# Moving four of the sixteen transposes of x1 from the output projection to the last product, and turning the order of the accumulator banks by one

## The chip, the cores and the metric

The kernel runs on one core of one Trainium2 chip. The metric is the device time of one execution in microseconds (us); the median of three executions counts. TensorE multiplies matrices and appears in a profile as PE (the matmuls) and PEld (the weight loads, LDWEIGHTS, that precede each matmul). DVE is VectorE, ACT is ScalarE, POOL is GpSimd, SP is SyncE, which issues the loads.

## What is computed

The reference is one decoder layer over 256 rows of width 1024, in float32:

```python
h = rmsnorm(x, norm1_g)
proj = h @ w_in                      # queries, keys, values, gates
y_nsa, y_moba = ...                  # two attention mixers
gm = sigmoid(g_m)                    # two merge gates of 1024 columns each
mixed = g_nsa * (y_nsa @ w_up_nsa) + g_moba * (y_moba @ w_up_moba)
x = x + mixed @ w_out                # x1 in what follows
h2 = rmsnorm(x, norm2_g)
u = relu(h2 @ w_ff1)                 # 1024 -> 4096
x = x + (u * u) @ w_ff2              # 4096 -> 1024, the last product
return rmsnorm(x, norm_f_g)
```

## The kernel before

Every weight matrix is cut into chunks of 128 x 2048 float32 (1 MB), in the order of the table `CHUNKS`. SP loads a chunk into a `raw` buffer. ACT rounds it to `whi` (type float32r, line 107) and DVE takes the rest `wlo = raw - whi` (line 109). There are three buffers of each, and chunk c+2 is split while chunk c is multiplied. Activations are kept as such pairs too: `hTh`/`hTl`, `mxh`/`mxl`, `h2h`/`h2l`, `sqh`/`sql`. One product is three matmuls (`mm3`, line 214): high by high, high by low, low by high; all matmuls of the products stand on line 212.

Two forms of product matter here. In the input projection and the last product the activation is the weight load and 512 columns of `whi` or `wlo` stream past. In the output projection (`wstat` and `two_blocks`, chunks `C_WOUT`, four of them, called wout 0 to 3) and in ff1 (chunks `C_FF1`, sixteen) it is the other way round: 128 columns of `whi` or `wlo` are the weight load, and the 256 columns of `mxh`/`mxl` or `h2h`/`h2l` stream past. Such a chunk has 48 matmuls of 256 columns, 24 for each of its two output blocks. In the last product (ff2, sixteen chunks) a chunk has 24 matmuls of 512 columns; its two last chunks are worked together, and their last 24 matmuls have 256 columns.

The order on each engine is written by hand. `run_slot` walks through a chunk's matmuls, and events that `at(pos, f)` has put down are called when the share `pos` of them has been issued; on PE they stand between two matmuls, on the other engines behind what was called before.

PSUM has eight banks. Four belong to the score tiles, and later to the last product; `yb` is one; `acc0`, `acc1` and `tp` are three. `tp` takes transposes up to the chunk before the merge gates: its last use is the second half of the keys `km`, which DVE reads last (line 312, `split_evac`). From the gates on it is one of three accumulators: `next_bank` (line 63) takes the first name of the list `turn["acc"]` and puts it at the end.

In wout 1 and in the second chunk of the last product, x1, which is held transposed as `x1T`, is turned back into rows by `x1_rows` (line 768): for each of four pairs of row blocks four 128 x 128 transposes on PE (line 773) into one bank, and one copy by ACT into `x1` (line 775). `rstd2` reads `x1` two chunks later.

Of the kernel before, what the change touches and what calls it, by code (L numbers as in the profile page):

```python
# [40 lines left out]
def hybrid_layer(ctx: ExitStack, tc: tile.TileContext, gxd, w, w1c, small, const, gf, out):  # L41
# [16 lines left out]
    def bank(tag, name):  # L58
        return ps.tile([128, 512], F32, name=name, tag=tag)

    turn = {"acc": ["acc0", "acc1"], "tp": ["tp", "yb"]}

    def next_bank(kind):
        t = turn[kind]
        t.append(t.pop(0))
        return bank(t[-1], kind)

    def acc_tile():
        return next_bank("acc")
# [6 lines left out]
    def s_tile(x):  # L76
        if "s" not in pools:
            early_stack.close()
            pools["s"] = at_stack.enter_context(tc.tile_pool(name="ps_s", bufs=1, space=PS))
        return pools["s"].tile([128, 2, 512], F32, name="S" + "ab"[x])  # L80
# [113 lines left out]
    def at(pos, f, *a):  # L194
        ev.append((pos, f, a))

    def run_slot(mms):
        n = len(mms)
        es = sorted(ev, key=lambda e: e[0])
        ev.clear()  # L200
        j = 0
        for i, m in enumerate(mms):
            while j < len(es) and es[j][0] <= i / n:
                es[j][1](*es[j][2])
                j += 1
            m()
        while j < len(es):
            es[j][1](*es[j][2])
            j += 1
# [24 lines left out]
    def wstat(o, c, off, nk, ncol, ah, al, ks=None, first=0, last=None):  # L234

        r = []
        last = nk - 1 if last is None else last
        for k in (range(nk) if ks is None else ks):
            a = k * ncol + off
            r += mm3(o, hi[c][:, a:a + 128], lo[c][:, a:a + 128], ah[:, k, :], al[:, k, :],  # L240
                     k == first, k == last)
        return r

    def split_events(c, hs, ls):
        for i in range(2):
            at(hs[i], split, c + 2, i, 2, "h")
        for i in range(2):
            if ls[i] <= 1:
                at(ls[i], split, c + 2, i, 2, "l")
        if ls[1] <= 1:  # L250
            at(max(ls) + 0.05, load, c + 5)

    def std_events(c):
        if 9 <= c < 20 and c % 2:
            split_events(c, (0.0, 0.06), (0.09, 0.46))
        elif 9 <= c < 20:
            split_events(c, (0.0, 0.45), (0.3, 0.8))
        else:
            split_events(c, (0.0, 0.45), (0.3, 0.46))
# [377 lines left out]
                       scale=hrstd[:, t:t + 1])  # L637

    prev = []
    turn["acc"].append("tp")  # L640
    for g in range(4):
        accs = [acc_tile(), acc_tile()]
        for i in range(2):
# [28 lines left out]
    def mix_t(t, i, tp):  # L672
        for j in range(4):
            pe.transpose(tp[:, j * 128:(j + 1) * 128],
                         sgs[0][:, t, (4 * i + j) * 128:(4 * i + j + 1) * 128], ident)
        k, q = mix_slices(t, i)
        U["mx", t, i] = tp.rearrange("p (j q) -> p j q", j=4)
        act.activation(mxh[:, k, q], U["mx", t, i], AF.Copy, scale=0.5)
# [35 lines left out]
    def two_blocks(c, ah, al, late=8):  # L714

        if late < 8:
            outs = [acc_tile()[:, 0:256] for _ in range(2)]
            whole = None
            order = [range(late), range(late, 8)]
        else:  # L720
            whole = acc_tile()
            outs = [whole[:, 0:256], whole[:, 256:512]]
            order = [range(8)]
        mms = []
        for ks in order:
            for m in range(2):
                mms += wstat(outs[m], c, m * 128, 8, 256, ah, al, ks=ks, last=7)
        return mms, outs, whole
# [34 lines left out]
    def lo_late(pos, c):  # L763
        for k in range(2):
            at(pos, split, c + 2, k, 2, "l")
        at(pos + 0.01, load, c + 5)

    def x1_rows(k2s, tiles):
        for k2, tp in zip(k2s, tiles):
            v = tp.rearrange("p (t d) -> p t d", t=2)  # L770
            for t in range(2):
                for m in range(2):
                    pe.transpose(v[:, t, m * 128:(m + 1) * 128],
                                 x1T[:, 2 * k2 + m, t * 128:(t + 1) * 128], ident)
            act.activation(FB["x1"][:, :, k2 * 256:(k2 + 1) * 256], v, AF.Copy)

    for i in range(4):
        c = C_WOUT + i
        if i == 0:
            at(0.03, lambda: mix_t(0, 1, bank("yb", "yb")))  # L780
            at(0.04, mix_l, 0, 1)
            at(0.29, lambda: mix_t(1, 1, s_tile(1)[:, 0]))
            at(0.3, mix_l, 1, 1)
            lo_late(0.35, c - 1)
        elif i == 1:
            lo_late(0.03, c - 1)
        split_events(c, (0.0, 0.1), ((9, 9), (0.3, 0.3), (0.3, 0.3), (9, 9))[i])
        for f, a in prev:
            at(0.02, f, *a)
        if i == 1:  # L790
            at(0.01, open_ff)

            at(26 / 48 - 0.001, lambda: x1_rows([0], [bank("yb", "yb")]))
            at(0.9, lambda: act.dma_start(FB["gfb"], gf[None, :].to_broadcast([128, 1024])))
        if i == 3:
            outs = [acc_tile()[:, 0:256] for _ in range(2)]
            at(0.52, wout_evac, i, outs, (0,))
            run_slot([m for j in range(2)
                      for m in wstat(outs[j], c, j * 128, 8, 256, mxh, mxl)])
            prev = [(wout_evac, (i, outs, (1,)))]  # L800
        else:
            mms, outs, _ = two_blocks(c, mxh, mxl, 4 if i == 0 else 8)
            run_slot(mms)
            prev = [(wout_evac, (i, outs))]
# [46 lines left out]
    def ff2_mms(i, p):  # L851
        c = C_FF2 + i
        t, c0, n = p
        r = []
        for k in range(2):
            kt = 2 * i + k
            lh, ll = (FB[a][:, kt, t * 128:(t + 1) * 128] for a in ("sqh", "sql"))
            a = k * 1024 + c0
            r += mm3(ops[p][:, 0:n], lh, ll, hi[c][:, a:a + n], lo[c][:, a:a + n],
                     kt == (28 if p == LAST[1] else 0),  # L860
                     kt == (27 if p == PARTS[1][1] else 31))
        return r
# [35 lines left out]
    for i in range(15):  # L898
        std_events(C_FF2 + i)
        for f, a in prev:  # L900
            at(0.02, f, *a)
        prev = []
        if i == 1:
            at(0.5, x1_rows, range(1, 4), [acc_tile() for _ in range(3)])
        if i == 3:
            at(0.1, rstd2)
        if i < 14:
            run_slot([m for p in order for m in ff2_mms(i, p)])
        else:
            ops[LAST[1]] = bank("yb", "yb")  # L910
            at(0.05, first_part)
            at(0.23, final_a, PARTS[0][0], 0)
            at(0.43, final_a, PARTS[0][1], 1)
            at(0.46, final_b, 0)
            at(0.64, final_a, PARTS[1][0], 0)
            at(0.83, final_a, LAST[0], 1)
            run_slot([m for p in PARTS[0] + PARTS[1][:1] + LAST for m in ff2_mms(14, p) + ff2_mms(15, p)])
# [87 lines left out]
```

## Time and profile before

| | |
|---|---|
| median of three executions | 386.05 us (385.52 to 386.81) |
| the profiled execution | 386.25 us, span 384.4 us |
| PE, matmuls | 375.2 us busy, 98% of the span |
| PEld, weight loads | 329.1 us, 86% |
| DVE | 254.3 us, 66% |
| ACT | 205.6 us, 54% |

The span runs from the first to the last instruction of the program, and 1.85 us lie outside it. A busy PE need not be PE at its peak: matmuls overlap, and a matmul's duration is longer than the distance between the starts of two. That distance is called the pitch below, and it is what a stream of matmuls costs.

### The profile page before, as it was taken

The page shows a single profiled execution, that of the slowest core. Times are in us where ns is not written, and L with a number is a line of the kernel's source. Part 1 is how long each engine was busy: PE and PEld are TensorE (multiplying, and loading weights), DVE is VectorE, ACT ScalarE, POOL GpSimd, SP SyncE. Part 2 cuts the span into 40 slices and gives each one's busy share as a digit, 9 for nine tenths or more (in the row PEclk, how much of TensorE's full clock was granted, in tenths as well). Part 3 has the DMA queues.
Part 4 walks back from the last instruction along what each step waited for, and adds up shares of the span by engine and source line. Part 5 has one row for each costly group of instructions (what it writes and reads, how often), then busy time and mean ns, then how long its engine had stood idle before and what let it go on. Part 6 is the DMA issues. An engine that isn't in the chain of part 4 may idle for free.

```text
span 384.4 us, 5939 instructions
## 1 busy us (share of the span) xinstructions
PE 375.2 (98%) x2404; PEld 329.1 (86%) x2404; DVE 254.3 (66%) x396; ACT 205.6 (54%) x359; POOL 3.2 (1%) x14
## 2 busy tenths in 40 slices
PE   7999999999999999999999999999999999999993
PEld 6897778878888788779999999999998888888883
DVE  3969788887966869567857656756757354344435
ACT  5974465766746747353554555565565364323412
POOL 1000000000000000000000000000000000000000
PEclk9999999999999999999999999999999999999999
DMA  7977535333533434630756644554564546545003
GB/s 243 368 304 231 208 124 205 109 111 124 206 109 112 124 140 175 217 112 7 264 224 219 220 160 175 215 188 155 206 213 143 206 186 237 198 162 188 0 2 110
DMA packets 11261, 66.31 MB, mean 173 GB/s; under 512 B 1249, under 2 KB 2785, under 8 KB 3937
## 3 DMA queue, kind: packets, MB, share of 16 engines
q1 hardware_dynamic: 10800, 65.14, 47.5%
q10 hardware_dynamic: 432, 0.79, 0.6%
q8 instruction: 19, 0.31, 0.3%
q14 instruction: 10, 0.07, 0.1%
HBM read 64.87 MB, written 1.05 MB: 172 GB/s over the span
## 4 chain that ended last, share of the span: by engine, by line
PE 90%; DVE 3%; ACT 2%; issue 2%; DMA 1%; SPq 1%; POOLq 0%; POOL 0%; DVEq 0%; ACTq 0%
PE acc L212 54%; PE o L212 21%; PE qacc L212 3%; PE yb L212 3%; PE kvbacc L212 2%; DMA raw<-in_kva_dram 1%; DVE wlo L109 1%; PE Sa L212 1%; PE Sa L493 1%; PE Sb L493 1%; ACT whi L107 1%; PE tp L293 1%; PE Sb L212 1%; PE tp L212 1%; DVE hTl L168 0%
## 5 line engine op out<-in xcount | busy, mean ns | idle before, releaser
L107 ACT ACTIVATE whi<-raw 128x1024 fp32r<-128x1024 f32 (+2 forms) x128 | 123.2, 991 | 99.6 <-PE o L212 35.5
L109 DVE TENSOR_TENSOR wlo<-raw,whi 128x1024 fp32r<-128x1024 f32 (+2 forms) x128 | 141.6, 1137 | 43.8 <-ACT whi L107 43.6
L212 PE MATMUL acc<-h2h,whi 128*128 128x256 f32 x256 | 71.9, 281 | 0.0
L212 PE MATMUL acc<-h2l,whi 128*128 128x256 f32 x256 | 71.9, 281 | 0.0
L212 PE MATMUL acc<-h2h,wlo 128*128 128x256 f32 x256 | 71.9, 281 | 0.0
L212 PE MATMUL acc<-whi,hTh 128*128 128x512 f32 (+1 forms) x128 | 51.2, 400 | 0.9 <-ACT whi L107 0.5
L212 PE MATMUL acc<-wlo,hTh 128*128 128x512 f32 (+1 forms) x128 | 51.1, 399 | 0.4 <-DVE wlo L109 0.2
L212 PE MATMUL acc<-whi,hTl 128*128 128x512 f32 (+1 forms) x128 | 49.8, 389 | 0.0
L212 PE MATMUL o<-whi,sqh 128*128 128x512 f32 (+1 forms) x128 | 49.5, 386 | 0.0
L212 PE MATMUL o<-whi,sql 128*128 128x512 f32 (+1 forms) x128 | 49.4, 386 | 0.0
L212 PE MATMUL o<-wlo,sqh 128*128 128x512 f32 (+1 forms) x128 | 49.4, 386 | 0.0
L212 PEld LDWEIGHTS acc<-h2h,wlo 128*128 128x128 f32 x256 | 49.2, 192 | 0.0
L212 PEld LDWEIGHTS acc<-h2h,whi 128*128 128x128 f32 x256 | 48.1, 188 | 0.0
L212 PEld LDWEIGHTS acc<-h2l,whi 128*128 128x128 f32 x256 | 48.1, 188 | 0.0
L212 PEld LDWEIGHTS acc<-whi,hTh 128*128 128x128 f32 x128 | 24.3, 190 | 7.9 <-ACT whi L107 1.3
L212 PEld LDWEIGHTS acc<-wlo,hTh 128*128 128x128 f32 x128 | 24.3, 190 | 5.4 <-DVE wlo L109 1.5
L212 PEld LDWEIGHTS o<-whi,sql 128*128 128x128 f32 x128 | 24.0, 188 | 4.9
L212 PEld LDWEIGHTS o<-wlo,sqh 128*128 128x128 f32 x128 | 24.1, 188 | 4.8
L212 PEld LDWEIGHTS o<-whi,sqh 128*128 128x128 f32 x128 | 24.0, 188 | 4.7
L212 PEld LDWEIGHTS acc<-whi,hTl 128*128 128x128 f32 x128 | 24.4, 190 | 4.2
L816 DVE TENSOR_TENSOR ur<-ur 128x512 f32<-128x512 f32 x16 | 11.1, 693 | 20.6 <-ACT ur L815 19.4
L818 DVE TENSOR_TENSOR sql<-ur,sqh 128x512 fp32r<-128x512 f32 x16 | 11.1, 692 | 11.2 <-ACT sqh L817 11.2
(245 smaller groups left out, 513.5 us busy)
## 6 DMA issues: line engine op xcount, KB each, us to landing
raw<-in_ff_dram SPq DMA_DIRECT2D x32, 1024.0 KB, 4.8
raw<-in_gm_dram SPq DMA_DIRECT2D x8, 1024.0 KB, 4.8
raw<-in_wout_dram SPq DMA_DIRECT2D x4, 1024.0 KB, 4.8
raw<-in_q_dram SPq DMA_DIRECT2D x2, 1024.0 KB, 5.9
raw<-in_qm_dram SPq DMA_DIRECT2D x2, 1024.0 KB, 5.3
raw<-in_km_dram SPq DMA_DIRECT2D x2, 1024.0 KB, 4.9
raw<-in_vm_dram SPq DMA_DIRECT2D x2, 1024.0 KB, 4.8
raw<-in_upn_dram SPq DMA_DIRECT2D x2, 1024.0 KB, 4.8
```

What stands on the lines that cost most here:

```text
L107: act.activation(hi[c][:, a:b], raw[c][:, a:b], AF.Copy)
L109: dve.tensor_tensor(lo[c][:, a:b], raw[c][:, a:b], hi[c][:, a:b].bitcast(F32), op=ALU.subtract)
L212: pe.matmul(o, l, r, start=start, stop=stop, skip_group_check=True)
L293: pe.transpose(tp[:, j * 256 + t * 128:j * 256 + t * 128 + 128], src[:, t, (2 * i + j) * 128:(2 * i + j + 1) * 128], ident)
L493: pe.transpose(S[x][:, j, c:c + 128], P[:, 2 * x + j, c:c + 128], ident)
L816: dve.tensor_tensor(rf, rf, rf, op=ALU.mult)
L818: dve.tensor_tensor(l, rf, h.bitcast(F32), op=ALU.subtract)
```

## The change

Three edits. The bank `tp` is put at the front of the list of accumulators instead of at its end, so that the first accumulator of the gates is in `tp`, and each later one in the bank that the accumulator before it had. The call of `x1_rows` in wout 1 goes. The call in the second chunk of the last product makes all four pairs, the last of them in the bank `yb`.

```diff
     prev = []
-    turn["acc"].append("tp")
+    turn["acc"].insert(0, "tp")
     for g in range(4):
...
         if i == 1:
             at(0.01, open_ff)
-
-            at(26 / 48 - 0.001, lambda: x1_rows([0], [bank("yb", "yb")]))
             at(0.9, lambda: act.dma_start(FB["gfb"], gf[None, :].to_broadcast([128, 1024])))
...
         if i == 1:
-            at(0.5, x1_rows, range(1, 4), [acc_tile() for _ in range(3)])
+            at(0.5, x1_rows, range(4), [acc_tile() for _ in range(3)] + [bank("yb", "yb")])
         if i == 3:
             at(0.1, rstd2)
```

PE where the gates begin, with the engine whose work each matmul waits for in brackets; `acc_961` is the first gates' accumulator, `acc_797` the last one of the values before it. Before:

```order
L212 MATMUL acc_797<-wlo_707,hTh_129 128x512
L212 MATMUL acc_797<-whi_706,hTl_130 128x512
L212 MATMUL acc_961<-whi_798,hTh_129 128x512 [waits Activation_49]
L212 MATMUL acc_961<-wlo_799,hTh_129 128x512
L212 MATMUL acc_961<-whi_798,hTl_130 128x512
```

Now:

```order
L212 MATMUL acc_797<-wlo_707,hTh_129 128x512
L212 MATMUL acc_797<-whi_706,hTl_130 128x512
L212 MATMUL acc_961<-whi_798,hTh_129 128x512 [waits DVE_49]
L212 MATMUL acc_961<-wlo_799,hTh_129 128x512
L212 MATMUL acc_961<-whi_798,hTl_130 128x512
```

No matmul has moved: the first one of the gates waits for DVE, where it waited for ACT.

PE in wout 1, at the start of its second block. Before:

```order
L212 MATMUL acc_1763<-mxh_1501,wlo_1651 128x256
L212 MATMUL acc_1763<-mxh_1501,whi_1650 128x256
L212 MATMUL acc_1763<-mxl_1502,whi_1650 128x256
L773 MATMUL yb_1826<-ident_72,gx_107 128x128 [waits DMAHW0_49,DVE_49]
L773 MATMUL yb_1826<-ident_72,gx_107 128x128 [waits DVE_49]
L773 MATMUL yb_1826<-ident_72,gx_107 128x128 x2
L212 MATMUL acc_1763<-mxh_1501,wlo_1651 128x256
L212 MATMUL acc_1763<-mxh_1501,whi_1650 128x256
L212 MATMUL acc_1763<-mxl_1502,whi_1650 128x256
```

Now the four transposes (`gx` holds x1T) are gone, and the chunk's 48 matmuls follow each other without a break, as those of wout 2, wout 3 and ff1 do before and now. PE in the second chunk of the last product, now:

```order
L212 MATMUL o0_512_2972<-whi_2910,sql_1781 128x512
L773 MATMUL acc_3012<-ident_72,gx_107 128x128 [waits DMAHW0_49,PE_49]
L773 MATMUL acc_3012<-ident_72,gx_107 128x128 x3
L773 MATMUL acc_3013<-ident_72,gx_107 128x128 [waits DMAHW4_49,PE_49]
L773 MATMUL acc_3013<-ident_72,gx_107 128x128 x3
L773 MATMUL acc_3014<-ident_72,gx_107 128x128 [waits DMAHW6_49,Activation_49]
L773 MATMUL acc_3014<-ident_72,gx_107 128x128 x3
L773 MATMUL yb_3015<-ident_72,gx_107 128x128 [waits DMAHW0_49]
L773 MATMUL yb_3015<-ident_72,gx_107 128x128 x3
L212 MATMUL o1_0_2973<-whi_2910,sqh_1780 128x512
```

Here sixteen transposes stand in a row between two 512-column matmuls, where there were twelve.

## Rows read from the trace of the kernel before

**Rows 1.** The profile's page, part 4: the chain that ended last, by engine.

```profile
PE 90%; DVE 3%; ACT 2%; issue 2%; DMA 1%; SPq 1%; POOLq 0%; POOL 0%; DVEq 0%; ACTq 0%
```

**Rows 2.** The chain of waits in order of time: start us, us, what.

```profile
31.00 1.99 PE tp L212 x64
...
179.08 5.85 PE acc L212 x49
184.93 0.44 PE yb L773 x4
185.36 104.35 PE acc L212 x886
...
297.88 1.31 PE acc L773 x12
299.19 73.48 PE o L212 x324
```

**Rows 3.** Timeline where the gates begin: start us, us, engine, line, operation [idle before].

```profile
85.40 0.68 DVE L312 TENSOR_TENSOR kml<-tp,kmh 128x512 fp32r<-128x512 f32 x1
...
85.56 0.39 PE L212 MATMUL acc<-whi,hTl 128*128 128x512 f32 x1
85.57 0.72 ACT L273 ACTIVATE vm<-acc,rstd 128x512 f32<-128x512 f32 x1
...
86.34 0.50 PE L212 MATMUL acc<-whi,hTh 128*128 128x512 f32 x1 [0.40 <-ACT vm L273]
```

**Rows 4.** Timeline of ACT in the last product's second chunk.

```profile
298.35 1.58 ACT L775 ACTIVATE x<-acc 128x512 f32<-128x512 f32 x3 [1.10 <-PE acc L773]
```

**Rows 5.** Timeline of PE in wout 1, around its transposes.

```profile
181.81 0.28 PE L212 MATMUL acc<-mxh,whi 128*128 128x256 f32 x1
...
184.53 0.28 PE L212 MATMUL acc<-mxh,whi 128*128 128x256 f32 x1
...
184.76 0.60 PE L773 MATMUL yb<-ident,gx 128*128 128x128 f32 x4
```

**Rows 6.** Groups of instructions, 179.7 to 184.6 us: xcount | busy us, mean ns.

```profile
L212 PE MATMUL acc<-mxh,wlo 128*128 128x256 f32 x15 | 4.1, 276 | 0.0
...
L212 PEld LDWEIGHTS acc<-mxh,wlo 128*128 128x128 f32 x15 | 2.8, 188 | 0.0
```

**Rows 7.** Groups of instructions, 199.2 to 289.2 us (ff1).

```profile
L212 PE MATMUL acc<-h2h,wlo 128*128 128x256 f32 x255 | 71.7, 281 | 0.0
L212 PEld LDWEIGHTS acc<-h2h,wlo 128*128 128x128 f32 x255 | 49.0, 192 | 0.0
...
L212 PEld LDWEIGHTS acc<-h2h,whi 128*128 128x128 f32 x255 | 47.9, 188 | 0.0
```

**Rows 8.** Busy us (xcount) of PE, PEld, DVE, ACT, POOL by stretch, granted clock, DMA.

```profile
181.00:184.60 3.60, 3.60 (x34) 3.60 (x33) 2.25 (x6) 2.70 (x4) 0.00 (x0) 1.00 0.60 189
...
240.00:245.00 5.00, 5.00 (x45) 5.00 (x44) 3.65 (x4) 2.48 (x4) 0.00 (x0) 1.00 0.57 213
```

**Rows 9.** Timeline of PE in wout 0, behind its second group of transposes (line 674).

```profile
177.07 0.60 PE L674 MATMUL Sb<-ident,sga 128*128 128x128 f32 x4
...
177.63 0.28 PE L212 MATMUL acc<-mxh,whi 128*128 128x256 f32 x1
...
178.65 0.28 PE L212 MATMUL acc<-mxh,whi 128*128 128x256 f32 x1
```

**Rows 10.** Timeline at the start of ff1, PE and DVE.

```profile
199.10 0.28 PE L212 MATMUL acc<-h2h,whi 128*128 128x256 f32 x1
...
200.30 0.48 DVE L759 SCALAR_TENSOR_TENSOR h2l<-gx,h2h 128x256 fp32r<-128x256 f32 x1 [0.58 <-ACT h2h L756]
...
200.70 1.22 DVE L109 TENSOR_TENSOR wlo<-raw,whi 128x1024 fp32r<-128x1024 f32 x1
```

**Rows 11.** Timeline of PE in the last 24 matmuls of the last product.

```profile
375.57 0.28 PE L212 MATMUL o<-whi,sqh 128*128 128x256 f32 x1
...
377.97 0.28 PE L212 MATMUL yb<-whi,sql 128*128 128x256 f32 x1
```

## The prediction

> **What bounds the kernel now.** I read the chain of waits first. PE holds 90% of it, DVE 3%, ACT 2% and loads 1% [rows 1]; so the time is what PE's stream costs, plus a few gaps. From 185.36 us on the chain is nothing but PE until the end of the last product: 886 matmuls, 36, twelve transposes, 324 [rows 2]. In this part no wait is to be had, and only a cheaper matmul can shorten it. Two places matter. The first is a gap where the gates begin. The second is the price of one matmul in wout and ff1, which I read as a pitch (start to start), since durations overlap.
>
> That price has two values for the same instruction. In wout 1, before its transposes, 24 matmuls lie between the start at 181.81 and the start at 184.53: 2.72 / 24 = 113.3 ns each [rows 5]. Behind the four transposes the chain has 886 matmuls in 104.35 us: 117.78 ns each [rows 2]. The count is exact: 22 left of wout 1, 48 in each of wout 2 and 3, 48 in each of sixteen chunks of ff1. The 512-column matmuls of the last product cost 73.48 / 324 = 226.8 ns, twice the lower value, so 113.3 is the rate of the stream and the other 4.4 ns are a loss. It is no matter of TensorE's clock: the granted clock is 1.00 (2.4 GHz) in a stretch at either pitch, and DVE, ACT and loads are busy in both [rows 8]. The weight loads tell more. At the lower pitch a load of `wlo` takes 188 ns and the matmul 276 [rows 6]; at the higher one the load of `wlo` takes 192, that of `whi` still 188, the matmul 281 [rows 7]. One load in three meets something in every round, and this has settled: it is there from the transposes to the end of ff1, whatever buffer is read. I take it for two steady states of the same stream, loads and streamed columns in step or out of step, and the transposes for what throws it from the one into the other.
>
> **The change part by part, against the profiled execution (386.25 us; the median is 0.20 lower).**
>
> *The gates' first accumulator.* Before, the last matmul of the values starts at 85.56, and the next was due a pitch later, at 85.79. It starts at 86.34, because ACT empties its bank only from 85.57 to 86.29 [rows 3]: a gap of 0.55 us. Now it waits for DVE's read of the keys in `tp`, 85.40 to 86.08 [rows 3]. With the same 0.05 us from end to start it begins at 86.13, a gain of 0.21 us. What stands in front of that read on DVE is not touched. Bounds: 0 if DVE runs 0.21 us later than in this execution, 0.55 if the read is done before PE comes. The second accumulator waits for the copy that ends at 86.29 and is due twelve pitches (2.7 us) after the first, so it is covered; all later accumulators only change names. PE's lead meets no load on the chain later, so I count it whole: -0.21.
>
> *The transposes on PE.* Four go, 0.44 us of the chain, and four come, in a row with twelve that take 1.31 us, 0.109 us each [rows 2]: -0.44 + 0.44 = 0. On ACT one copy moves along, behind the three of the last product, 1.58 / 3 = 0.53 us each [rows 4]. They stand between the roundings of two chunks, and what hides the fourth is the rest of the chunk on PE, twelve matmuls of 226.8 ns, 2.7 us; without that cover it would cost at most its 0.53 us, once. The `yb` bank is idle there, and `rstd2` comes two chunks later. The load of the last gain vector is issued on ACT a little earlier, without the copy before it, and is used only at the end. All nothing.
>
> *The pitch.* If the stream stays at 113.3 ns through the rest of wout and through ff1, 886 x (117.78 - 113.33) = 3.94 us go. No row shows ff1 at the lower pitch, so I bound it: from above by this 3.94, from below by a loss, if the stream goes to the pitch of the last product's 256-column matmuls. There 20 lie between 375.57 and 377.97, 120.0 ns each [rows 11], and 886 x 2.2 = 2.0 us would be added. I take the upper end, by the nearest row: the same matmuls with the same operands as the 22 next, directly before them, with nothing between. In wout the good state crosses a seam unharmed: it is there from 179.7 on, in wout 0, and wout 1 begins at 181.81 with other buffers and another bank [rows 5, 6].
>
> Against it: transposes alone don't decide the state. Behind the second group in wout 0 nine steps from 177.63 to 178.65 take 1.02 us, 113.3 ns again [rows 9]. So there is chance in how a break ends, and a later break could do what this one did. I find none: the 22 + 96 + 768 matmuls stand in one row, and what feeds them is early. The last `h2l` ends at 200.78 [rows 10], 1.7 us after ff1 begins; it is wanted 36 matmuls in, 4.1 us at the lower pitch. The next chunk's `wlo` comes from the first two of the splits from 200.70 on, 1.22 us each [rows 10]; both are done 4.0 us after ff1's start and are wanted from 5.4 us on. A chunk of ff1 would take 48 x 113.3 ns = 5.44 us, just what a chunk of the last product takes now (24 x 226.8 ns) with the same 1 MB load. DVE, 3.65 of 5 us busy in ff1 [rows 8], would be at 76%.
>
> The Trainium skill, "TensorE: Matmul & The Clock Gate", section "Step-by-step: what each phase is for", speaks against this: PE has two independent read ports in SBUF, so that loading the next weights takes nothing from the running matmul. By it, load and stream could not disturb each other, the 4.4 ns would have a cause that the transposes don't touch, and the sum would be the first rival's. The trace does not agree as far as it shows: the load of `wlo` is 4 ns longer exactly where the matmul is 5 ns longer [rows 6, 7].
>
> Sum: 386.25 - 0.21 - 3.94 = 382.10 for the profiled execution, **381.9 us** against the median.
>
> **The rivals.**
>
> 1. *The pitch stays at 117.8.* The transposes only happen to stand where the stream leaves its short good stretch; or it falls back at the next seam, at the latest where `h2h` takes the place of `mxh`. For: the good state is seen for at most the 49 matmuls before the transposes [rows 2], and never with `h2h`. Against: its stretch ends at the transposes to the matmul, not at a seam. Left is the gap at the gates: 386.05 - 0.21 = 385.8; if only wout keeps the lower pitch, (22 + 96) x 4.45 ns = 0.5 us more go, 385.3. Here the change does little of what it could.
>
> 2. *PE's queue feeds it no faster.* Two instructions per 117.78 ns, 58.9 each, would be the limit, and the quicker stretches would live off what was stored in a wait. That too gives 385.8. Against it: 64 matmuls with their 64 loads pass in 1.99 us at 31.0 us [rows 2], 15.5 ns per instruction. The skill's same page, section "Wait — 56ns, not 53.3ns?", states about 62 ns per matmul for one way of decoding; the 1.99 us exclude that here.
>
> 3. *The stream stays good into ff1 and falls back in the middle of it:* 382.5 to 384.9.
>
> 4. *Slower: the stream settles at 120 ns*, the third value, which the last product's final matmuls take up within three matmuls, without any transposes [rows 11]. It decides at the first seam behind wout 1's first half. 886 x 2.2 ns = 2.0 us more, less 0.21: 387.8. Against: there the roles are others, the activation is the load and `whi` streams, and all three loads are slow, not one.
>
> **How the numbers follow.** Forecast 0.64; rival 1 0.21; rival 2 0.03; rival 3 0.06; rival 4 0.06. A measurement can tell about 0.3%, 1.16 us, from no change: faster means below 384.9. The forecast and rival 3 lie there: 0.70. Rivals 1 and 2 are no change: 0.24. Rival 4 is slower: 0.06. The range reaches from 381.2 (the forecast, 0.34 more at the gates if DVE is done early, and 0.4 for the spread of a median between 385.5 and 386.8) to 386.1 (rivals 1 and 2 with the gain at the gates at 0), and leaves out rival 4. The forecast's own range is 381.2 to 382.5.
>
> **What would show it.** Right: the chain's 864 matmuls of wout 2, wout 3 and ff1, if not more, cost 113.3 ns each, their loads of `wlo` take 188 ns and the matmuls 276; the gates' first matmul follows DVE's read of `kml` with about 0.35 us of gap left; sixteen transposes take some 1.75 us in the last product. Wrong: `wlo` loads of 192 ns in ff1 (rival 1), in all three loads (rival 4), or a wait for `whi`, `wlo` or a load inside ff1, which would say that the quicker stream outruns what feeds it.

## The result, and the profile after

| | before | after |
|---|---|---|
| median | 385.64 us (385.50 to 386.81, 6 executions) | 381.88 us (381.43 to 382.69, 6 executions) |
| ratio, 95% interval | | 0.9893 [0.9876, 0.9910] |
| the profiled execution | 386.25 us, span 384.4 us | 382.69 us, span 380.8 us |

Faster by 1.1%, more than three times what a measurement can tell from no change; 381.9 us had been forecast. The chain of waits of the changed kernel, in order of time (start us, us, what), answers to [rows 2]:

```profile
178.72 0.70 DVE mxl L682
179.43 0.04 issue
179.47 106.25 PE acc L212 x935
285.72 8.18 PE o L212 x36
293.90 1.31 PE acc L773 x12
295.21 0.44 PE yb L773 x4
295.65 73.48 PE o L212 x324
```

Where there were 49 matmuls, four transposes and 886 matmuls, there are 935 matmuls in a row. From the end of the wait for `mxl` to the first matmul of the last product PE needs 106.25 us, where it needed 5.85 + 0.44 + 104.35 = 110.64 [rows 2]. Of the 4.39 us that are gone, 0.44 are the four transposes, which come back at 295.21, and 3.95 are a cheaper matmul. The 36 and 324 matmuls of the last product cost what they did. Groups of instructions in ff1, 199 to 286 us (xcount | busy us, mean ns of one), which answer to [rows 7]:

```profile
L212 PE MATMUL acc<-h2h,wlo 128*128 128x256 f32 x256 | 70.7, 276 | 0.0
...
L212 PEld LDWEIGHTS acc<-h2l,whi 128*128 128x128 f32 x255 | 47.9, 188 | 0.0
L212 PEld LDWEIGHTS acc<-h2h,wlo 128*128 128x128 f32 x255 | 47.9, 188 | 0.0
L212 PEld LDWEIGHTS acc<-h2h,whi 128*128 128x128 f32 x254 | 47.7, 188 | 0.0
```

All loads take 188 ns; the `wlo` load of 192 ns is gone, and with it the matmul of 281. The clock has no part in it, as before: the stretches 180 to 198 and 200 to 284 us (busy us and count of PE, PEld, DVE, ACT, POOL, then the granted clock, the DMA share and GB/s) stand at 1.00 (2.4 GHz), and 84 us hold 744 matmuls, those that overlap the edges among them, where [rows 2] stand for 84 / 0.11778 = 713:

```profile
180.00:198.00 18.00, 18.00 (x161) 18.00 (x160) 14.22 (x22) 9.06 (x13) 0.00 (x0) 1.00 0.75 264
200.00:284.00 84.00, 84.00 (x744) 84.00 (x743) 57.39 (x64) 48.46 (x63) 0.00 (x0) 1.00 0.56 196
```

The timeline where the gates begin answers to [rows 3]:

```profile
85.98 0.68 DVE L312 TENSOR_TENSOR kml<-tp,kmh 128x512 fp32r<-128x512 f32 x1
...
86.14 0.39 PE L212 MATMUL acc<-whi,hTl 128*128 128x512 f32 x1
86.16 0.72 ACT L273 ACTIVATE vm<-acc,rstd 128x512 f32<-128x512 f32 x1
...
86.72 0.50 PE L212 MATMUL acc<-whi,hTh 128*128 128x512 f32 x1 [0.18 <-DVE kml L312]
```

The first matmul of the gates was due at 86.14 + 0.23 = 86.37, waits for DVE's read of `tp` and starts at 86.72: a gap of 0.35 us, where it was 0.55. The profiled execution is still 0.6 us longer than the 382.10 worked out for it. This lies ahead of the stretch above, whose start is 0.39 us later than before and not 0.21 earlier. PE's list of waits names what came in between: before, one wait of 0.5 us for a rounding to `whi`; in this execution,

```profile
PE acc L212 <- ACT whi L107: 1.4, 2, 0.9
PE acc L212 <- DVE kml L312: 0.2, 1, 0.2
PE acc L212 <- DVE mxl L682: 0.2, 1, 0.2
```

(us in total, times, longest). The chain shows this rounding at 77.20 us, in a part that the change does not touch; it varies between executions, and 382.69 is the longest of the six.

### The profile page after: what moved, and what is told of

It reads as the page before. It is cut to its first block, busy times and chain, and to the rows that moved or that the text cites. A ratio compares the mean times of both kernels' runs of the same rounds, so it can differ in the third digit from the quotient of the medians.

```text
span 380.8 us, 5938 instructions
## 1 busy us (share of the span) xinstructions
PE 370.8 (97%) x2404; PEld 324.8 (85%) x2404; DVE 254.3 (67%) x396; ACT 205.7 (54%) x359; POOL 3.2 (1%) x14
## 4 chain that ended last, share of the span: by engine, by line
PE 87%; DVE 5%; ACT 2%; issue 2%; DMA 1%; SPq 1%; POOLq 0%; POOL 0%; DVEq 0%; ACTq 0%
PE acc L212 52%; PE o L212 21%; PE kvbacc L212 2%; PE yb L212 2%; DVE wlo L109 2%; PE qacc L212 2%; ACT whi L107 2%; DMA raw<-in_kva_dram 1%; PE Sa L493 1%; PE Sb L493 1%; PE Sa L212 1%; PE tp L212 1%; PE Sb L212 1%; PE tp L293 1%; DVE hTl L168 0%
## 5 line engine op out<-in xcount | busy, mean ns | idle before, releaser
L212 PE MATMUL acc<-h2h,whi 128*128 128x256 f32 x256 | 70.7, 276 | 0.0
L212 PE MATMUL acc<-h2l,whi 128*128 128x256 f32 x256 | 70.7, 276 | 0.0
L212 PE MATMUL acc<-h2h,wlo 128*128 128x256 f32 x256 | 70.7, 276 | 0.0
L212 PE MATMUL acc<-whi,hTh 128*128 128x512 f32 (+1 forms) x128 | 50.8, 397 | 1.6 <-ACT whi L107 1.4
L212 PE MATMUL acc<-wlo,hTh 128*128 128x512 f32 (+1 forms) x128 | 50.7, 396 | 0.4 <-DVE wlo L109 0.2
L212 PE MATMUL o<-whi,sqh 128*128 128x512 f32 (+1 forms) x128 | 49.5, 386 | 0.0
L212 PE MATMUL acc<-whi,hTl 128*128 128x512 f32 (+1 forms) x128 | 49.4, 386 | 0.0
L212 PE MATMUL o<-whi,sql 128*128 128x512 f32 (+1 forms) x128 | 49.4, 386 | 0.0
L212 PE MATMUL o<-wlo,sqh 128*128 128x512 f32 (+1 forms) x128 | 49.4, 386 | 0.0
L212 PEld LDWEIGHTS acc<-h2h,whi 128*128 128x128 f32 x256 | 48.1, 188 | 0.0
L212 PEld LDWEIGHTS acc<-h2l,whi 128*128 128x128 f32 x256 | 48.1, 188 | 0.0
L212 PEld LDWEIGHTS acc<-h2h,wlo 128*128 128x128 f32 x256 | 48.1, 188 | 0.0
L212 PEld LDWEIGHTS acc<-whi,hTh 128*128 128x128 f32 x128 | 24.1, 189 | 8.4 <-ACT whi L107 2.1
L212 PEld LDWEIGHTS acc<-wlo,hTh 128*128 128x128 f32 x128 | 24.1, 188 | 5.4 <-DVE wlo L109 1.6
L212 PEld LDWEIGHTS o<-whi,sql 128*128 128x128 f32 x128 | 24.0, 188 | 4.9
L212 PEld LDWEIGHTS o<-wlo,sqh 128*128 128x128 f32 x128 | 24.0, 188 | 4.8
L212 PEld LDWEIGHTS o<-whi,sqh 128*128 128x128 f32 x128 | 24.0, 188 | 4.8
L212 PEld LDWEIGHTS acc<-whi,hTl 128*128 128x128 f32 x128 | 24.1, 188 | 4.2
```

Of the source, the lines that this page charges most:

```text
L212: pe.matmul(o, l, r, start=start, stop=stop, skip_group_check=True)
```

## Experiments

Below, **quick** is a stream of 256-column matmuls at 113.3 ns from start to start, **slack** one at 117.8 ns, and a **break** is whatever stands between two such matmuls: a wait, or transposes. The question was whether the transposes alone make the stream slack, or any break may, or the place in the program does. Over all experiments the kernel before was executed 51 times on three chips, between 385.32 and 387.71 us.

**1. The bank alone** (kernel before, one edit):

```diff
-    turn["acc"].append("tp")
+    turn["acc"].insert(0, "tp")
```

> The bank order alone; the x1 transposes stay where they were. Theory (two steady states, the four transposes in wout 1 throw the stream from 113.3 to 117.8 ns): the gap before the gates' first matmul shrinks from 0.55 to about 0.35 us, the 886 matmuls behind the transposes still cost 117.8 ns each, and the median is 0.2 us below before, about 385.4. Rival (the good pitch of ff1 comes from the accumulators' other banks, not from the transposes): 113.3 ns from the transposes on as well, about 381.9.

385.79 us (385.21 to 387.73, 10 executions), ratio 0.9999 [0.9981, 1.0018]. The 0.2 us is too small to be seen in the time; in the trace the gap at the gates is 0.34 us (due at 85.53 + 0.23 = 85.76, start at 86.10). The chain of waits held something else:

```profile
178.10 0.70 DVE mxl L682
178.80 0.04 issue
178.84 6.04 PE acc L212 x49
184.88 0.44 PE yb L773 x4
185.32 104.35 PE acc L212 x886
```

The 49 matmuls between the wait for `mxl` and the transposes take 6.04 us, where they took 5.85 [rows 2]: here the stream is slack ahead of the transposes already. So the transposes are not needed for it. PE's wait for `mxl` in wout 0 is a break of 0.43 us (start to start) too, and the stream behind it may be either.

**2. The transposes of x1 alone** (the changed kernel with its first edit undone):

```diff
-    turn["acc"].insert(0, "tp")
+    turn["acc"].append("tp")
```

> The move of the four x1 transposes alone; banks as before. Theory: 113.3 ns from wout 1 to the end of ff1, weight loads of wlo 188 ns, 3.9 us below before, about 381.7 to 382.1; the gates' gap stays 0.55 us. Rival (the banks do it): 117.8 ns, about 385.6.

The ten executions fall into two groups with nothing between: 381.49, 381.63, 381.97, 382.00, 382.89 and 385.70, 385.97, 386.51, 386.66, 386.96; ratio of the medians 0.9957 [0.9918, 0.9996], which describes neither. The groups lie 4.5 us apart by their middle values (381.97 and 386.51); 935 matmuls at 4.45 ns are 4.2. Only one of the ten has a trace; it was quick, with the same row `106.25 PE acc L212 x935` as the change. So it looks as if each execution takes one of the two values of the pitch and keeps it (this is called a draw below); that the slower five were slack from the wait for `mxl` on is inferred from the distance between the groups.

**3. One break in the middle of ff1** (the changed kernel, one group of four transposes moved from the last product into ff1's chunk 8; the last product keeps the other three):

```diff
+        if i == 8:
+            at(26 / 48 - 0.001, lambda: x1_rows([0], [bank("yb", "yb")]))
```

> The changed kernel, but the first four x1 transposes stand in ff1 chunk 8 behind its 26th matmul, as they stood in wout 1. Theory: 113.3 ns up to them, 117.8 ns with wlo loads of 192 ns in the 358 matmuls (22 + 7 x 48) behind them; 358 x 4.45 ns = 1.6 us slower than the changed kernel, about 383.4. Rival (only something in wout 1, such as the mxh operands or the work of the other engines there, made the bad state; the transposes are harmless in ff1): 113.3 ns on both sides, about 381.9.

385.22 us, one execution. It could not answer: its chain is slack from the wait for `mxl` on.

```profile
177.96 68.23 PE acc L212 x577
246.19 0.44 PE yb L773 x4
246.63 42.17 PE acc L212 x358
```

68.23 / 577 = 118.2 ns, which counts a step of 0.22 us at the exit of the wait (behind it the starts are 117.8 ns apart), and 42.17 / 358 = 117.8. What it did show: the same program as the change up to chunk 8 can leave that wait slack.

**4. Fourteen breaks** (the changed kernel with the same four transposes done again in ff1's chunks 1 to 14, behind 13 to 38 of the chunk's 48 matmuls):

```diff
+    BREAKS = {1: 26, 2: 25, 3: 26, 4: 27, 5: 26, 6: 14, 7: 26, 8: 28, 9: 26, 10: 38, 11: 26, 12: 13, 13: 26, 14: 15}
...
+        n = BREAKS.get(i)
+        if n:
+            at(n / 48 - 0.001, lambda: x1_rows([0], [bank("yb", "yb")]))
```

> The changed kernel with four more transposes (x1_rows of pair 0 again, into yb) in each of the ff1 chunks 1 to 14, behind matmul 26, 25, 26, 27, 26, 14, 26, 28, 26, 38, 26, 13, 26, 15 in turn. Each break costs its own 0.44 us, 6.2 us in all. Theory A (a break decides anew between the states, by where among the three matmuls of a product it stands): the pitch between breaks takes both values; behind matmul 26 it is 117.8, behind other places it can be 113.3, also right after a stretch at 117.8. Theory B (any break of this kind throws the stream into the bad state, nothing takes it out): 117.8 ns from the first break, behind matmul 26 of chunk 1, to the end of ff1. Either way 388 to 392 us.

389.08 us, one execution. Its chain, from the first breaks:

```profile
178.25 27.59 PE acc L212 x241
205.84 0.44 PE yb L773 x4
206.28 5.54 PE acc L212 x47
211.82 0.44 PE yb L773 x4
212.25 5.58 PE acc L212 x49
217.83 0.44 PE yb L773 x4
218.26 5.78 PE acc L212 x49
```

Two rows of 49 matmuls stand there, 5.58 and 5.78 us: quick and slack, (5.78 - 5.58) / 49 = 4.1 ns apart. Distances of starts, from the first matmul behind a break on (ns), and the mean from the seventh on:

```
section          n   first six                  mean
206.03..211.53  47   201 117 118 118 118 117   117.80
212.01..217.55  49   207 118 114 113 113 114   113.33
230.22..234.29  36   201 117 117 123 118 114   113.31
278.11..282.29  37   201 120 116 116 114 114   113.33
```

Behind the wait for `mxl` and the fourteen breaks the stream was, in order: quick, slack, quick, slack, slack, quick, slack, quick, slack, slack, quick, quick, quick, quick, quick. So a break can turn quick into slack, slack into quick, or leave either; within at most six matmuls it is settled, and nothing changed it until the next break. The place in the chunk does not decide: of the seven breaks behind 26 matmuls four left the stream quick and three slack.

**5. The change again**, unedited, on another chip.

> The changed kernel once more, many executions. The runs so far put the choice of state at the 0.43 us wait for mxl in wout 0: with one and the same program before it, its exit was followed by 113.3 ns in some profiles and 117.8 ns in others, and the move of the x1 transposes alone gave five executions near 382 and five near 386. Theory (each execution draws its state at that wait, whatever the banks): some executions lie near 381.4 to 382.7 and some, 10 to 50%, near 385.5, with nothing between. Rival (the turned banks settle the draw): all executions within 381.4 to 382.9.

382.04 us (381.51 to 382.50, 4 executions), ratio 0.9898 [0.9883, 0.9913]: all quick.

**6. and 7. The streamed operand elsewhere in SBUF** (the changed kernel; two filler tiles ahead of and behind `h2h` and `h2l` set where these begin, in steps of 4 bytes a partition). Number 6 puts them 64 bytes further, number 7 puts them 32 bytes further; what lies behind them stays where it was.

```diff
-        p.tile([128, 96], F32, name="gap")
+        p.tile([128, 112], F32, name="gap")
...
-        p.tile([128, 16], F32, name="gap2")
```

(Number 7: 104 and 8.)

> The changed kernel with h2h and h2l 64 bytes further on in SBUF, so that they begin on a multiple of 128 bytes as whi and wlo do; nothing else moves. Theory (weight load and streamed columns collide in SBUF, and their relative place decides which states there are): ff1 takes another steady pitch, most likely the 120 ns of the last product's final matmuls, whose operands both begin on multiples of 128 bytes: 768 x 6.7 ns = 5.1 us slower than the changed kernel's good state, about 387. Rival (place plays no part): 113.3 or 117.8 ns as before, 381.9 or 385.5.

> The changed kernel with h2h and h2l 32 bytes further on. Theory (place decides): a pitch in ff1 that is the same for all 768 matmuls whatever state wout was in, and that may differ from 113.3, 117.8 and 120. Rival (place plays no part): the state of wout 1 to 3 goes on through ff1 unchanged.

Number 6 took 388.49 us and number 7 385.67, one execution each. In both, wout is quick, and ff1 is neither quick nor slack. Groups of number 6, 206 to 286 us:

```profile
L212 PE MATMUL acc<-h2h,whi 128*128 128x256 f32 x223 | 63.1, 283 | 0.0
...
L212 PEld LDWEIGHTS acc<-h2h,whi 128*128 128x128 f32 x223 | 42.8, 192 | 0.0
L212 PEld LDWEIGHTS acc<-h2l,whi 128*128 128x128 f32 x223 | 42.8, 192 | 0.0
L212 PEld LDWEIGHTS acc<-h2h,wlo 128*128 128x128 f32 x222 | 42.6, 192 | 0.0
```

The timeline at ff1's start settles within nine steps: 119, 112, 117, 118, 119, 121, 117, 117 ns, then 120 to the end. All three loads are slow, as in the matmuls of [rows 11], of whose loads the trace of the kernel before has (375.6 to 378 us)

```profile
L212 PEld LDWEIGHTS yb<-whi,sqh 128*128 128x128 f32 x4 | 0.8, 192 | 0.0
```

There `sqh` and `whi` both begin at a multiple of 128 bytes, as `h2h`, `whi` and `wlo` do here; in the kernel as it is, `h2h` and `h2l` begin 64 bytes behind such a multiple. (This is worked out from the sizes of the kernel's tiles, taking each to begin at a multiple of 32 bytes; the traces hold no addresses.) The chain has 111.35 us for the 935 matmuls: 111.35 - 106.25 = 5.10 us more, 768 x 6.64 ns in ff1. In number 7 the steps go round between 115 and 123 ns to the end and never settle; 110.08 us, (110.08 - 106.25) / 768 = 5.0 ns more each. There the matmuls take 281 ns, as in the slack stream, but all loads take 188 on average (187 to 191), as in the quick one (a piece of the chain, then the loads of `wlo` from 206 to 286 us):

```profile
178.67 110.08 PE acc L212 x935
```

```profile
L212 PEld LDWEIGHTS acc<-h2h,wlo 128*128 128x128 f32 x226 | 42.6, 188 | 0.0
```

Nothing but the place of the streamed operand was changed, and with it the pitch, and in number 6 the duration of the loads, which read another operand. So load and stream do disturb each other, and the place has a part in which pitches there are; each place was run once. Whether it is the place itself or that against the weights', these two runs do not tell.

**8. and 12. Without the waits** (the changed kernel; the keys' last read earlier; in wout 0 the second transposes behind the 10th matmul in place of the 14th, number 12 behind the 11th, and the second half of that chunk's rounding later, so that `mxl` should be there in time):

```diff
-            split_events(c, (0.0, 0.06), (0.09, 0.46))
+            split_events(c, (0.0, 0.06), (0.09, 0.49 if c == 11 else 0.46))
...
-            at(0.29, lambda: mix_t(1, 1, s_tile(1)[:, 0]))
-            at(0.3, mix_l, 1, 1)
+            at(0.2, lambda: mix_t(1, 1, s_tile(1)[:, 0]))
+            at(0.21, mix_l, 1, 1)
...
-        split_events(c, (0.0, 0.1), ((9, 9), (0.3, 0.3), (0.3, 0.3), (9, 9))[i])
+        split_events(c, (0.0, 0.3 if i == 0 else 0.1), ((9, 9), (0.3, 0.3), (0.3, 0.3), (9, 9))[i])
```

(Number 12: 0.22 and 0.225.)

> The changed kernel with two waits of PE taken away: the second transposes of wout 0 stand four matmuls earlier and ACT rounds the second half of a chunk behind them and not ahead, so that mxl is there in time; and at the gates DVE reads the keys before, not after, it splits half a chunk. Theory (the state is drawn at the exit of the wait for mxl): without that wait no draw, the good state that followed the transposes of wout 0 in all six profiles so far goes on to the end of ff1 in every execution: 0.4 us for the wait and 0.35 us for the gates below the good state of the changed kernel, all executions within 380.4 to 382. Rival (any break draws): the transposes alone now draw, and executions lie both near 381 and near 385.

> As the kernel without the two waits, which was in the bad state in all of its 11 executions, but with the second transposes of wout 0 one matmul later, behind the 11th, where DVE has sga ready. There they began behind a wait of some 0.1 us, and the bad state followed. Theory (a break whose transposes themselves don't wait, and that stands behind a good state, leads on into the good state as the ones behind the 14th matmul did every time): 113.3 ns to the end of ff1, about 381.2 in all executions. Rival (what the break draws can't be told from where it stands): 117.8 ns, about 385.4, in all or some of them.

Number 8: 385.67 us (385.15 to 386.89, 11 executions), ratio 0.9999 [0.9989, 1.0009], although PE's waits for `kml` and `mxl` are gone from the trace. Its chain is

```profile
175.93 0.55 PE Sb L674 x4
176.48 111.89 PE acc L212 x950
```

111.89 / 950 = 117.8 ns. The earlier transposes wait for `sga`:

```profile
175.07 0.69 DVE L667 TENSOR_TENSOR sga<-sga,sgb 128x512 f32<-128x512 f32 x1
...
175.82 0.66 PE L674 MATMUL Sb<-ident,sga 128*128 128x128 f32 x4
```

They start at 175.82, 0.17 us behind the start of the matmul ahead of them, since DVE ends `sga` only at 175.76; what they left was slack, and no later break followed that could have turned it back. Number 12: two groups again, 381.65, 381.72, 382.01, 382.78 and eight from 385.10 to 386.69, median 385.5, ratio 0.9958 [0.9930, 0.9987]. In its profiled execution the transposes leave a quick stream, and with the 15th matmul behind them it turns slack. The timeline there, DVE and PE:

```profile
178.69 0.69 DVE L682 SCALAR_TENSOR_TENSOR mxl<-Sb,mxh 128x512 fp32r<-128x512 f32 x1 [0.52 <-ACT mxh L678]
...
179.34 0.28 PE L212 MATMUL acc<-mxh,whi 128*128 128x256 f32 x1
179.43 0.19 PEld L212 LDWEIGHTS acc<-mxl,whi 128*128 128x128 f32 x1
179.46 0.36 PE L212 MATMUL acc<-mxl,whi 128*128 128x256 f32 x1
179.54 0.19 PEld L212 LDWEIGHTS acc<-mxh,wlo 128*128 128x128 f32 x1
179.66 0.28 PE L212 MATMUL acc<-mxh,wlo 128*128 128x256 f32 x1
```

DVE ends `mxl` at 179.38; the load of the weights for the matmul that reads it starts at 179.43, the matmul itself still starts 0.11 us behind the one ahead, and the step behind it is 0.20 us, as behind a break. A delay of under 0.1 us was enough, and the list of waits does not even name it. Two waits were taken away, 0.31 us for `mxl` (0.43 less a step) and 0.35 us at the gates, and the time grew: by 3.6 us in number 8 (385.67 - 382.04, the change on the same chip, number 5) and by 3.9 us in the eight slower executions of number 12 (their median 385.88 - 381.96, number 10).

**9. The transposes of x1 alone, again**, on a third chip (number 2, unedited).

> The move of the x1 transposes alone, a second time, on the same chip and beside the changed kernel. On another chip it gave five executions at 381.5 to 382.9 and five at 385.7 to 387.0. Theory (the draw at the wait for mxl depends on the chip or on chance, not on the banks): the share of executions near 386 is like that of the changed kernel in the same call, few or none for both or some for both. Rival (the turned banks settle the draw): some near 386 here, none in the changed kernel.

382.48 us (381.62 to 383.26, 6 executions), ratio 0.9901 [0.9884, 0.9918]: all quick, where five of ten were slack before. The names of the banks do not settle the draw.

**10. The change a third time**, same chip as number 9.

> The changed kernel beside the run before, same chip. So far ten of ten executions lay at 381.4 to 382.7. Theory (chance or chip): the same share near 385.5 as with the x1 move alone. Rival (banks): none.

381.96 us (381.74 to 382.44, 5 executions), ratio 0.9892 [0.9877, 0.9908].

**11. The keys read first** (the changed kernel; on DVE the read of `tp` ahead of half a split):

```diff
-            split_events(c, (0.0, 0.06), (0.09, 0.46))
+            split_events(c, (0.0, 0.06), (0.09, 0.49 if c == 11 else 0.46))
```

> The changed kernel, with DVE's read of the keys ahead of the half split of a chunk that stood before it. Theory (the first gates' matmul waits for that read alone): the gap at the gates goes, 0.35 us below the changed kernel where both are in the good state, about 381.6. The wait for mxl stays, so the state is drawn as in the changed kernel. Rival (the chunk half that is split later is late itself): PE waits for wlo two chunks on, and nothing is won.

382.05 us (381.39 to 383.27, 6 executions), ratio 0.9896 [0.9878, 0.9914]. The gap at the gates is closed:

```profile
85.97 0.39 PE L212 MATMUL acc<-whi,hTl 128*128 128x512 f32 x1
86.20 0.39 PE L212 MATMUL acc<-whi,hTh 128*128 128x512 f32 x1
86.42 0.39 PE L212 MATMUL acc<-wlo,hTh 128*128 128x512 f32 x1
```

Against number 10, on the same chip, no gain shows in the time: the executions of one kernel lie up to 1.9 us apart, and its profiled one holds 1.9 us of waits for `whi` against 1.0 in number 10's. No version was found that is faster than the change.

## Why the prediction was right

**The pitch** was the forecast's large term, -3.94 us by 886 x (117.78 - 113.33 ns), and -3.95 came: the stream stays quick from the wait for `mxl` through three seams of wout, the change from `mxh` to `h2h`, and all of ff1. The reading behind it held too: two steady states of one stream, the loads of `wlo` telling them apart, and a break as what throws it. Experiment 4 shows both states inside ff1 within one execution, with nothing but breaks between. That load and stream disturb each other is borne out by number 6; that the two states are these two in and out of step is still a picture, which no run shows.

**The gates**: -0.21 us was expected and the gap went from 0.55 to 0.35 us. It is shown at its place only; in the time 0.2 us could not be resolved (experiments 1 and 11). That PE's lead there meets nothing later was therefore neither confirmed nor refuted.

**The transposes**: +0.44 - 0.44. The four came back at 295.21 for 0.44 us, and the last product's other matmuls are unchanged. Confirmed.

**Rival 1** (the pitch stays at 117.8): it is not what the change gave, but it was more than a rival; it is the other outcome of the same draw. It came in five of ten executions of number 2, by their times, and in number 3. **Rival 2** (PE's queue) is excluded: 864 matmuls of wout 2 and 3 and ff1 at 113.3 ns behind a single wait cannot live off a store, and number 6 shows 120 ns by the place of an operand alone. **Rival 3** (it falls back inside ff1) has no trace: in no profile of these operands at their place did the stream change between two breaks (in numbers 6 and 7 it changed where the moved `h2h` came in). **Rival 4** (120 ns) did not come, but exists for these operands at another place (number 6). The rule that speaks against the change, of the Trainium skill, "TensorE: Matmul & The Clock Gate", section "Step-by-step: what each phase is for" (loading the next weights takes no SBUF read bandwidth from the running matmul), would, as the prediction took it, leave the stream undisturbed by the loads, and that is not what was measured: with the operand moved 64 bytes, loads go from 188 to 192 ns and matmuls from 276 to 283. Where the two meet, no run shows.

**What the prediction missed.** Its step "there is chance in how a break ends, and a later break could do what this one did. I find none" looked only behind wout 1's transposes. The break that now decides stands ahead of them: the wait for `mxl`. I had taken the quick state behind it as given, since [rows 5, 6] show it in one execution; experiments 1 and 3 show it slack at the same place. The change removed the break that left the stream slack in every execution of the kernel before, and put the end of the stream in the hands of the wait before it. In the change that wait was left quick in 15 of 15 timed executions. But the slack exits that were seen at it (numbers 1, 2 and 3) all came on one chip, on which the unedited change was not timed in these experiments. The forecast had no term for such a draw, so that its number came true is in part luck: where number 2 ran, which differs from the change in the bank alone, half of the executions took about the time of rival 1.

**Open**: what decides a draw. A place has a strong leaning: slack behind wout 1's transposes in all 51 executions, by their times, quick behind the wait for `mxl` in 10 of the 12 traces that have it. It is neither the place in the chunk (number 4) nor the bank (number 9; numbers 1 and 3 were slack with the turned banks). Two things go with the outcome. The first step behind a group of transposes was 205 to 207 ns in 18 cases over all traces, and each of these 18 streams was quick; it was 200 to 202 ns in 27, of which 17 were quick and 10 slack. So the outcome shows already in a few ns of that step; what sets it is not shown. And the wait for `mxl`, by traces and times, was left slack in 7 of 13 executions on the chip of numbers 1 to 4, and in none of 23 on the other two. So much makes one common chance unlikely, but the kernels were not the same in all of these, and whether it was the chip, the runs do not separate.

## What to carry to other kernels

Where the same instruction shows two prices, compare their pitch and the durations of the loads on both sides of every break in the stream, waits included; a break can cost 4% of the hundreds of matmuls behind it, far more than its own length. Count breaks in a long stream of short matmuls, put those that must be there where matmuls are longer, and time such a kernel in many executions on more than one chip, because two groups of times hide behind one median. Try also where the streamed operand begins: 64 bytes were worth 5 us here, in the one execution that was made.

## What was not expected of the hardware

- A stream of 256-column matmuls, each with its own load, has several steady pitches, 113.3 and 117.8 ns at one place of its operand, 120.0 at another 64 bytes on, and a cycle of 115 to 123 at 32 bytes. It keeps one for 950 matmuls, 112 us.
- A delay of under 0.1 us can move it from one pitch to the other (number 12), and a break of 0.44 us can move it back (number 4).
- The 512-column stream does not keep what a break leaves: 324 matmuls behind twelve transposes [rows 2] and behind sixteen take the same 73.48 us, 226.8 ns each.
